# The modulation weights of a transformer block, loaded as whole megabytes two or three units ahead, and the norms' sums ahead of the units beside them

## The chip, the cores and the metric

The kernel runs on one core of a Trainium2 chip. The metric is the time of one execution on the device, in microseconds (us); a kernel's number is the median of its runs. PE is the matmul engine (TensorE), DVE is VectorE, ACT is ScalarE, POOL is GpSimd, and SP (SyncE) issues the loads. L387 is line 387 of the kernel before.

## The reference

Two blocks stand one behind the other, each of two layers, on 256 tokens `x` and 256 context tokens of width 1024. The change lies in the second block. Its first layer (i = 2 in the kernel) mixes by attention over 8 heads, its second (i = 3) by pooling over windows; both have a feed-forward part with a short convolution. Six vectors of modulation come for each layer from a matrix product of the condition `c`:

```
m = (silu(c) @ w_mod[i] + b_mod[i])           # 1024 -> 6 x 1024, also for the context's c
shift_m, scale_m, gate_m, shift_f, scale_f, gate_f = six parts of m
h = rmsnorm(x, g_pre_mix[i]) * (1 + scale_m) + shift_m
y = attention(h, hc) @ w_o    (i = 2)    or    pool_mix(h, w_pool)    (i = 3)
x = x + gate_m * rmsnorm(y, g_post_mix[i])
h = rmsnorm(x, g_pre_ffn[i]) * (1 + scale_f) + shift_f
x = x + gate_f * rmsnorm(conv_ffn(h, w_up, conv_w, conv_b, w_down), g_post_ffn[i])
```

## The kernel before

Everything is held with features on the 128 partitions: `x` is 8 tiles of 128 x 256. Weights arrive in fp32, mostly in pieces of 512 KB (`w`, L224), and are split into a high part `wh` (ACT, L238) and the rest `wl` (DVE, L240); a product is three matmuls, high by high (L285), high by low (L286 or L289) and low by high. The activations are split the same way, `hH` on ACT and `hL` on DVE or POOL (`h_tile`).

*Units.* The modulation of a layer is worked out in 24 units of 256 columns. A unit reads 1 MB of `w_mod` as two halves of 512 KB (`mod_half`, tile `mw`, three buffers, L375), multiplies it by the padded condition in 8 matmuls (L387; the trace counts 16, as fp32 goes in two passes), copies the result on ACT (`modsb`, L390), transposes it twice on PE (L396), and reduces it and adds the bias on DVE (L398, L400). `mod_units` gives a list of calls: with `ahead=1` call q issues the load of unit q and the matmuls of unit q - 1. The load is issued inside the unit, behind the copy. Units with `x8=True` take the megabyte in one DMA into a big buffer (`wm`, L366) out of a pool of seven that `y`, `sx`, the split activations and large weights share; the first block's first units are loaded so.

*Order.* The orders of PE and SP are written by hand: they are those in which the Python code issues instructions. `Line` interleaves several generators: a generator yields a cost in us, which moves a clock forward, and a wait, the time after which it is due again. The orders of ACT, DVE and POOL are set by a scheduler. All loads of weights and of units go out on SP's queue in SP's order, and SP waits at a load until the load's buffer is free.

*Where the units stand.* In the attention of layer 2 (`attention2`) 12 units of layer 3 are spread over the heads: `kx`, `vx`, `q` are the projections, `un[hp]` the scores (L1178), softmax (DVE L625, ACT L1184, DVE L1188), transposes of P (L635) and products with v (L1198) of a pair of heads. The other 12 are `self.late`; they stand beside three norms: behind the attention (post 1, five calls), behind the feed-forward of layer 2 (post 2, four) and behind the pool mixer (post 3, the rest).

*A norm* (`post_norm`) joins `rmsnorm(y)` to `x` and makes the next `h`. It needs sums over features, made by matmuls with ones: the squares of y (L449, L450) give `rstd` on ACT and DVE (L463 to L468); two more sums (L1076, of `x*y` and `y*y` with the gain, added up in `self.sx`) give the correction `m` (L1078 to L1080) to the stored sum of squares of x (L1081), and from that the second `rstd`. So h can start without a pass over the new x. `post_x` applies y to the tiles of x, five of them on POOL (L1107, L1108) and the others on DVE. In post 3 the sums of `x*y` are made in the pool mixer (L1282). `post` starts the norm's generator and runs the units beside it:

```
def post(self, units, *args):
    self.go(self.post_norm(*args), "p")
    self.run(units)
    self.line.ensure("p")
```

Of the kernel before, what the change touches and what calls it, by code (L numbers as in the profile page):

```python
# [105 lines left out]
class Stack:  # L106
# [853 lines left out]
    def ffn(self, i, T, streams, after):  # L960
# [3 lines left out]
        post = i >= 2  # L964
# [66 lines left out]
        for q in streams:  # L1031
            for ft in range(KD):
                self.go(down(len(groups) - 1, ft, slice(256 * q, 256 * q + 256)))
            after(q, nst[q], y)


# [28 lines left out]
    def post_norm(self, i, y, st, j, g):  # L1065


        nc = self.nc
        yield 0, 1.2
        ry = self.rstd(st)  # L1070
        yield 0.9, 1.5
        ps = st.get("S")
        if ps is None:
            ps = self.psum("S", [P, 2, 512])
            for n in range(2):
                nc.tensor.matmul(ps[:, n, :NT], lhsT=self.ones, rhs=self.sx[:, 1 + n], start=True, stop=True)  # L1076
        m, sx = self.t1k("m"), self.sx[:, 0]
        nc.vector.tensor_tensor(m, ps[:, 1, :NT], ry, ALU.mult)  # L1078
        nc.vector.scalar_tensor_tensor(m, ps[:, 0, :NT], 2.0, m, ALU.mult, ALU.add)
        nc.vector.tensor_tensor(m, m, ry, ALU.mult)  # L1080
        im = nc.vector.tensor_tensor(sx, sx, m, ALU.add)  # L1081
        for ft in st["pool"]:
            self.post_x(y, ry, st, ft)
        rx = self.rstd_of(sx)
        ir = self.last
        if (i, j) == (3, 3):
            self.gate = ir.ins, 1
        with self.tc.issue_after(im.ins):
            self.post_x(y, ry, st, 0)

        def pre(ft):
            if ft and ft not in st["pool"]:
                with self.tc.issue_after(ir.ins):
                    self.post_x(y, ry, st, ft)

        yield 0, 6
        yield from self.h_split(i, j, g, rx, 0, pre, POOL_H2)
        yield 0.9, 0
# [54 lines left out]
    def attention2(self):  # L1153
        nc, i, line = self.nc, 2, self.line
# [55 lines left out]
        kx, vx = chunk(0, lambda acc, s: self.post_k(acc, s, tk)), chunk(1, self.post_v)  # L1210
        q = [chunk(2 + c, post_q(c)) for c in range(4)]
        un = units()
        f = self.more_units((3, 0, 12))
        seq = kx + vx + q[0] + q[1] + need("c0", "c1", "c2") + f[:2]
        seq += spread(un[0], f[2:5]) + q[2] + need("c3") + spread(un[1], f[5:7]) + q[3] + need("c4")
        seq += spread(un[2], f[7:10]) + need("c5") + spread(un[3], f[10:])
        seq += need(*(f"a{hp}1" for hp in range(4)))
        for u in seq:
            u()
# [14 lines left out]
        for cc in range(4):  # L1234
            for f2 in range(2):
                self.go(wo(cc, f2))
        return y, nst

    def pool_consts(self):
# [11 lines left out]
    def pool_mixer(self):  # L1251
# [33 lines left out]
        nst["S"] = self.psum("S", [P, 2, 512])  # L1285
        for n in (0, 1, -1, -2, 2, -3, -4, 3, -5, -6, -7, -8):
            self.go(z(n) if n >= 0 else out(-n - 1), f"z{n}")
        line.ensure(*(f"z{-n - 1}" for n in range(KD)))
        return y, nst

# [11 lines left out]
            return self.mod_units(1, range(0, 12), True)  # L1302
        return self.more_units((2, 8, 24)) if i == 1 else []

    def more_units(self, *parts):
        return self.mod_units(None, [(i, n) for i, a, b in parts for n in range(a, b)])

    def post(self, units, *args):

        self.go(self.post_norm(*args), "p")  # L1310
        self.run(units)
        self.line.ensure("p")

    def run(self, units):
# [68 lines left out]
    def build_all(self):  # L1383
# [19 lines left out]
        if self.upto == "L1":  # L1403
            return self.finish()

        self.late = self.more_units((3, 12, 24))
        y, st = self.attention2()
        self.post(self.late[:5], 2, y, st, 3, self.sm("sm2", "n2g"))
        self.pool_consts()

        def after2(q, st, y):
            self.post(self.late[5:9], 3, y, st, 0, self.sm("sm3", "n1g"))

        self.ffn(2, 256, (0,), after2)
        if self.upto == "S0":
            return self.finish()
        y, st = self.pool_mixer()
        self.post(self.late[9:], 3, y, st, 3, self.sm("sm3", "n2g"))

        def after3(q, st, y):  # L1420
            self.go(self.post_last(y, st), "p")
# [155 lines left out]
```

## Time and profile before

| | |
|---|---|
| median of 3 runs | 1829.44 us (1826.78 to 1840.67) |
| the profiled execution | 1839.73 us |
| its span in the trace | 1837.9 us |
| mean granted clock of PE | 0.946 |
| PE busy | 1650.7 us, 90% |
| DVE, ACT, POOL busy | 64%, 49%, 7% |
| moved by DMA | 288.39 MB, 157 GB/s |
| chain that ended last | PE 65%, DVE 13%, DMA 13%, ACT 6% |
| loads of `mw`, 512 KB, x152 | median 5.0 us from issue to landing |
| loads of `wm`, 1024 KB, x20 | median 7.7 us |

The times of the trace are those of the one profiled execution, and start at its first instruction. The second block's attention lies at 1195 to 1327, post 1 behind it, post 2 at 1559 to 1585, post 3 at 1607 to 1630. The granted clock is a share of the full speed of 2.4 GHz; at any moment PE runs at this or at half of it. "Idle before <-releaser" is how long an engine stood before the instruction and what it waited for last.

### The profile page before, as it was taken

Reading aid. Unit: us, or ns where it says so; the run is one execution under the profiler, and the core shown is the slowest. Engines: PE = TensorE matmul, PEld = TensorE weight load, DVE = VectorE, ACT = ScalarE, POOL = GpSimd, SP = SyncE. Lnnn points to the kernel's source line nnn. Section 1 sums busy time; section 2 is a strip of 40 time slices with the busy share of each in tenths; the row PEclk is TensorE's granted clock in tenths of the full one; section 3 lists DMA queues with packets and bytes.
Section 4 is the critical chain, followed back from the end, with each engine's and each line's share of the span. In section 5 each row is a group of like instructions: output and inputs, shape, how many; then the busy total and the mean of one; then the engine's idle time right before and its main releaser. Section 6 shows DMA issues by size and latency. Waiting matters only on the chain.

```text
span 1837.9 us, 32872 instructions
## 1 busy us (share of the span) xinstructions
PE 1650.7 (90%) x12736; PEld 1443.7 (79%) x12736; DVE 1180.2 (64%) x2992; ACT 900.9 (49%) x2213; POOL 133.0 (7%) x162
## 2 busy tenths in 40 slices
PE   6999797999999998897799999969779999769997
PEld 5877457989889898874488888856659998459997
DVE  5665786656554567865688576746556567666665
ACT  5445554534333334554456464534446565546563
POOL 1000001000000000000001011000221012221010
PEclk9999898999999999997989999989969999789998
DMA  7334330433334332355627767465455544345552
GB/s 310 102 138 152 108 123 24 138 136 117 114 117 138 115 117 70 121 201 184 220 96 280 247 220 246 132 218 172 131 191 173 186 167 155 124 152 188 178 193 84
DMA packets 74892, 288.39 MB, mean 157 GB/s; under 512 B 8560, under 2 KB 9840, under 8 KB 69104
## 3 DMA queue, kind: packets, MB, share of 16 engines
q1 hardware_dynamic: 73152, 283.91, 45.3%
q10 hardware_dynamic: 1584, 2.38, 0.4%
q8 instruction: 100, 1.64, 0.4%
q14 instruction: 56, 0.46, 0.1%
HBM read 285.21 MB, written 1.05 MB: 156 GB/s over the span
## 4 chain that ended last, share of the span: by engine, by line
PE 65%; DVE 13%; DMA 13%; ACT 6%; issue 2%; POOL 1%; SPq 0%; ACTq 0%; DVEq 0%; POOLq 0%
PE S L285 9%; PE S L286 9%; PE S L289 9%; PE acc L285 8%; PE acc L289 8%; PE acc L286 8%; DMA mw<-in_wmod_dram 5%; DVE wl L240 4%; DMA w<-in_wup_dram 4%; PE acc L387 4%; DMA w<-in_wdn_dram 3%; ACT wh L238 2%; DVE ht L493 1%; PE tr L635 1%; PE tr L396 1%
## 5 line engine op out<-in xcount | busy, mean ns | idle before, releaser
L240 DVE TENSOR_TENSOR wl<-w,wh 128x384 fp32r<-128x384 f32 (+2 forms) x1010 | 488.0, 523 | 249.8 <-ACT wh L238 224.4
L238 ACT CAST wh<-w 128x384 fp32r<-128x384 f32 (+2 forms) x1010 | 419.8, 475 | 313.1 <-PE S L286 88.3
L285 PE MATMUL S<-hH,wh 128*128 128x256 f32 x1408 | 350.3, 286 | 20.6 <-ACT hH L503 13.6
L286 PE MATMUL S<-hL,wh 128*128 128x256 f32 x1408 | 348.4, 285 | 4.2 <-POOL hL L501 2.8
L285 PEld LDWEIGHTS S<-hH,wh 128*128 128x128 f32 x1408 | 270.7, 192 | 27.4 <-ACT hH L503 14.4
L286 PEld LDWEIGHTS S<-hL,wh 128*128 128x128 f32 x1408 | 270.5, 192 | 6.5 <-POOL hL L501 3.5
L285 PE MATMUL acc<-gH,wh 128*128 128x256 f32 (+1 forms) x728 | 209.9, 312 | 13.8 <-DVE xc L944 5.5
L286 PE MATMUL acc<-gL,wh 128*128 128x256 f32 (+1 forms) x728 | 205.3, 306 | 0.0
L289 PE MATMUL S<-hH,wl 128*128 128x256 f32 x1408 | 198.3, 284 | 0.0
L289 PEld LDWEIGHTS S<-hH,wl 128*128 128x128 f32 x1408 | 182.5, 193 | 0.0
L285 PEld LDWEIGHTS acc<-gH,wh 128*128 128x128 f32 x728 | 138.8, 191 | 29.3 <-DVE x L944 5.9
L387 PE MATMUL acc<-mw,cpad 128*32 128x256 f32 x1216 | 95.8, 427 | 60.9 <-DMA mw<-in_wmod_dram 60.4
L289 PE MATMUL acc<-gH,wl 128*128 128x256 f32 (+1 forms) x728 | 146.0, 306 | 0.0
L286 PEld LDWEIGHTS acc<-gL,wh 128*128 128x128 f32 x728 | 139.0, 191 | 5.7
L289 PEld LDWEIGHTS acc<-gH,wl 128*128 128x128 f32 x728 | 110.4, 191 | 6.5
L387 PEld LDWEIGHTS acc<-mw,cpad 128*32 128x32 f32 x1216 | 31.6, 115 | 105.9 <-DMA mw<-in_wmod_dram 51.5
L955 DVE SCALAR_TENSOR_TENSOR cgv<-S,sm,cgv 128x255 f32<-128x255 f32 (+1 forms) x132 | 74.9, 568 | 39.5 <-ACT cgv L952 39.1
L285 PE MATMUL acc<-wh,hH 128*128 128x256 f32 x344 | 92.4, 299 | 7.5 <-ACT hH L503 5.5
L390 ACT COPY modsb<-acc 128x256 f32<-128x256 f32 x96 | 35.5, 370 | 127.0 <-PE acc L387 126.3
L952 ACT ACTIVATE cgv<-S,sm 128x256 f32<-128x256 f32 (+1 forms) x132 | 82.8, 627 | 24.8 <-PE S L289 24.8
L993 POOL TENSOR_TENSOR gL<-cgv,gH 128x256 fp32r<-128x256 f32 x66 | 51.7, 783 | 543.6 <-ACT gH L992 525.7
L286 PE MATMUL acc<-wl,hH 128*128 128x256 f32 x344 | 88.6, 288 | 0.0
(261 smaller groups left out, 3011.2 us busy)
## 6 DMA issues: line engine op xcount, KB each, us to landing
mw<-in_wmod_dram SPq DMA_DIRECT2D x152, 512.0 KB, 5.0
w<-in_wup_dram SPq DMA_DIRECT2D x140, 512.0 KB, 4.1
w<-in_wdn_dram SPq DMA_DIRECT2D x56, 512.0 KB, 3.7
wm<-in_wmod_dram SPq DMA_DIRECT2D x20, 1024.0 KB, 7.7
w<-in_wup_dram SPq DMA_DIRECT2D x18, 1024.0 KB, 7.6
w<-in_win_dram SPq DMA_DIRECT2D x32, 512.0 KB, 4.2
w<-in_wout_dram SPq DMA_DIRECT2D x16, 512.0 KB, 5.5
w<-in_wqkv_dram SPq DMA_DIRECT2D x16, 512.0 KB, 4.2
```

The source lines that it names most:

```text
L238: self.nc.scalar.copy(h[:, c:d], w[:, c - a:d - a])
L240: self.nc.vector.tensor_tensor(l[:, c:d], w[:, c - a:d - a], h[:, c:d].bitcast(F32), ALU.subtract)
L285: mm(o, lhsT=s[0], rhs=m[0], start=k == ks[0], stop=False)
L286: mm(o, lhsT=s[0], rhs=m[1], start=False, stop=False)
L289: mm(o, lhsT=S(b, k)[1], rhs=M(b, k)[0], start=False, stop=end and k == ks[-1])
L387: nc.tensor.matmul(acc[32 * q:32 * q + 32], lhsT=cpad[:, k], rhs=w[k // 4][:, q], start=k < 4, stop=k >= 4)
L390: nc.scalar.copy(sb, acc)
L396: nc.tensor.transpose(tr[:, t].rearrange("p q v -> p (q v)"), sb[:, P * t:P * t + P], self.ident)
L493: nc.vector.scalar_tensor_tensor(t, self.xs[s][:, ft], A, r, ALU.mult, ALU.mult)
L952: nc.scalar.activation(out, ps, AF.Identity, scale=cw[:, n + f:n + f + 1], bias=cb[:, f:f + 1])
L955: nc.vector.scalar_tensor_tensor(o[:, :, 1:256], x[:, :, 0:255], cw[:, f:f + 1], o[:, :, 1:256], ALU.mult, ALU.add)
L993: (nc.vector if T == 512 else nc.gpsimd).tensor_tensor(gL[:, a], c[:, 1, :T], gH[:, a].bitcast(F32), ALU.subtract)
```

## The change

All 24 units of layer 3 are loaded whole, one DMA of 1 MB each, into the pool of seven big buffers. In the attention they are asked for two units ahead: the first load stands before the projection of k, the second behind that of v, and no unit's matmuls stand ahead of the first scores. The late units become three groups of four, three ahead. A group's first three loads are issued by `early_loads` at tiles 3, 4 and 5 of the loop ahead of each norm (output projection, last part of the down projection, output of the pool mixer), and its fourth in the first unit. `post` then runs the units alone. In `post_norm` the two sums have shorter waits in `Line`, which puts them earlier in PE's row. The weights, products and results are the same.

```diff
--- before.py
+++ after.py
@@ -1031,6 +1031,8 @@
         for q in streams:
             for ft in range(KD):
                 self.go(down(len(groups) - 1, ft, slice(256 * q, 256 * q + 256)))
+                if i == 2:
+                    self.early_loads(ft)
             after(q, nst[q], y)
 
 
@@ -1066,9 +1068,9 @@
 
 
         nc = self.nc
-        yield 0, 1.2
+        yield 0, 0.8
         ry = self.rstd(st)
-        yield 0.9, 1.5
+        yield 0.9, 0.8
         ps = st.get("S")
         if ps is None:
             ps = self.psum("S", [P, 2, 512])
@@ -1210,10 +1212,10 @@
         kx, vx = chunk(0, lambda acc, s: self.post_k(acc, s, tk)), chunk(1, self.post_v)
         q = [chunk(2 + c, post_q(c)) for c in range(4)]
         un = units()
-        f = self.more_units((3, 0, 12))
-        seq = kx + vx + q[0] + q[1] + need("c0", "c1", "c2") + f[:2]
-        seq += spread(un[0], f[2:5]) + q[2] + need("c3") + spread(un[1], f[5:7]) + q[3] + need("c4")
-        seq += spread(un[2], f[7:10]) + need("c5") + spread(un[3], f[10:])
+        f = self.more_units((3, 0, 12), x8=True, ahead=2)
+        seq = f[:1] + kx + vx + f[1:2] + q[0] + q[1] + need("c0", "c1", "c2")
+        seq += spread(un[0], f[2:5]) + q[2] + need("c3") + spread(un[1], f[5:8]) + q[3] + need("c4")
+        seq += spread(un[2], f[8:11]) + need("c5") + spread(un[3], f[11:])
         seq += need(*(f"a{hp}1" for hp in range(4)))
         for u in seq:
             u()
@@ -1234,6 +1236,7 @@
         for cc in range(4):
             for f2 in range(2):
                 self.go(wo(cc, f2))
+                self.early_loads(2 * cc + f2)
         return y, nst
 
     def pool_consts(self):
@@ -1285,6 +1288,8 @@
         nst["S"] = self.psum("S", [P, 2, 512])
         for n in (0, 1, -1, -2, 2, -3, -4, 3, -5, -6, -7, -8):
             self.go(z(n) if n >= 0 else out(-n - 1), f"z{n}")
+            if n < 0:
+                self.early_loads(-n - 1)
         line.ensure(*(f"z{-n - 1}" for n in range(KD)))
         return y, nst
 
@@ -1302,13 +1307,19 @@
             return self.mod_units(1, range(0, 12), True)
         return self.more_units((2, 8, 24)) if i == 1 else []
 
-    def more_units(self, *parts):
-        return self.mod_units(None, [(i, n) for i, a, b in parts for n in range(a, b)])
-
-    def post(self, units, *args):
-
+    def more_units(self, *parts, **kw):
+        return self.mod_units(None, [(i, n) for i, a, b in parts for n in range(a, b)], **kw)
+
+    def early_loads(self, ft):
+
+        if 3 <= ft < 6 and self.late:
+            self.late[0][ft - 3]()
+
+    def post(self, *args):
+
+        units = self.late.pop(0)
         self.go(self.post_norm(*args), "p")
-        self.run(units)
+        self.run(units[3:])
         self.line.ensure("p")
 
     def run(self, units):
@@ -1403,19 +1414,19 @@
         if self.upto == "L1":
             return self.finish()
 
-        self.late = self.more_units((3, 12, 24))
+        self.late = [self.more_units((3, n, n + 4), x8=True, ahead=3) for n in (12, 16, 20)]
         y, st = self.attention2()
-        self.post(self.late[:5], 2, y, st, 3, self.sm("sm2", "n2g"))
+        self.post(2, y, st, 3, self.sm("sm2", "n2g"))
         self.pool_consts()
 
         def after2(q, st, y):
-            self.post(self.late[5:9], 3, y, st, 0, self.sm("sm3", "n1g"))
+            self.post(3, y, st, 0, self.sm("sm3", "n1g"))
 
         self.ffn(2, 256, (0,), after2)
         if self.upto == "S0":
             return self.finish()
         y, st = self.pool_mixer()
-        self.post(self.late[9:], 3, y, st, 3, self.sm("sm3", "n2g"))
+        self.post(3, y, st, 3, self.sm("sm3", "n2g"))
 
         def after3(q, st, y):
             self.go(self.post_last(y, st), "p")
```

SP's row in the attention, before (-) and after (+): `wqkv` and `wo` are the weights of the projections, `wmod` those of the units.

```order
-L224 DMA w<-in_wqkv_dram 128x1024 x14
-L375 DMA mw<-in_wmod_dram 128x1024 x10
+L224 DMA w<-in_wqkv_dram 128x1024 x6
+L366 DMA wm<-in_wmod_dram 128x2048
+L224 DMA w<-in_wqkv_dram 128x1024 x4
+L366 DMA wm<-in_wmod_dram 128x2048
+L224 DMA w<-in_wqkv_dram 128x1024 x4
+L366 DMA wm<-in_wmod_dram 128x2048 x3
 L224 DMA w<-in_wo_dram 128x1024 x2
-L375 DMA mw<-in_wmod_dram 128x1024 x4
+L366 DMA wm<-in_wmod_dram 128x2048 x3
 L224 DMA w<-in_wo_dram 128x1024 x2
```

Ten half-megabyte loads stood behind all qkv weights; now two whole ones stand among these and three behind them.

PE's row in the attention before, from the last transposes of the first queries (L584) to the last unit ahead of the third query projection:

```order
L584 MATMUL tr<-cst,rp_13265 128x128 x4
L387 MATMUL acc<-mw,cpad_104 32x256 x8
L1178 MATMUL S<-kv,qT 128x512 x2
L396 MATMUL tr<-cst,modsb 128x128 x2
L387 MATMUL acc<-mw,cpad_104 32x256 x8
L1178 MATMUL S<-kv,qT 128x512 x2
L584 MATMUL tr<-cst,rp_13360 128x128 x4
L396 MATMUL tr<-cst,modsb 128x128 x2
L387 MATMUL acc<-mw,cpad_104 32x256 x16
```

And after, the same place (L1180 is the line of the scores there):

```order
L584 MATMUL tr<-cst,rp_13269 128x128 x4
L1180 MATMUL S<-kv,qT 128x512 x2
L387 MATMUL acc<-wm,cpad_104 32x256 x8
L1180 MATMUL S<-kv,qT 128x512 x2
L396 MATMUL tr<-cst,modsb 128x128 x2
L584 MATMUL tr<-cst,rp_13364 128x128 x4
L387 MATMUL acc<-wm,cpad_104 32x256 x16
```

The first scores stood behind a unit and now stand ahead of all of them; four units stood here, now three.

PE's row at post 2, before (-) and after (+), behind the last matmuls of the down projection; post 1 reads the same.

```order
-L387 MATMUL acc<-mw,cpad_104 32x256 x16
+L387 MATMUL acc<-wm,cpad_104 32x256 x8
 L449 MATMUL tr<-nacc,ones 128x256
 L450 MATMUL tr<-sq,ones 128x256
-L396 MATMUL tr<-cst,modsb 128x128 x4
-L387 MATMUL acc<-mw,cpad_104 32x256 x16
-L1076 MATMUL S<-sx,ones 128x256 x2
+L387 MATMUL acc<-wm,cpad_104 32x256 x8
+L396 MATMUL tr<-cst,modsb 128x128 x2
+L1078 MATMUL S<-sx,ones 128x256 x2
+L387 MATMUL acc<-wm,cpad_104 32x256 x8
+L396 MATMUL tr<-cst,modsb 128x128 x2
```

The sums of the squares of y stood behind two units and now stand behind one; the sums of `self.sx` stood behind two more and now stand behind one more.

## Rows read from the trace of the kernel before

**Rows 1.** stages: us, PE, PEld, DVE, ACT, POOL busy (x); clock; DMA; GB/s
```profile
1195.00:1320.00 125.00, 100.17 (x712) 75.34 (x712) 68.39 (x194) 51.10 (x130) 4.91 (x6) 0.90 0.52 173
1320.00:1368.00 48.00, 29.84 (x185) 21.13 (x184) 26.52 (x66) 20.56 (x49) 17.49 (x22) 0.70 0.58 190
```

**Rows 2.** attention, idle of PE before L387: releaser, us, times
```profile
  DMA mw<-in_wmod_dram: 21.7, 6
```

**Rows 3.** waits of PE, 1545 to 1670: releaser, us, times, longest
```profile
PE acc L387 <- DMA mw<-in_wmod_dram: 14.7, 4, 5.9
```

**Rows 4.** post 1, PE in order: start, length, instruction, [idle before <-releaser]
```profile
1333.48 2.23 PE L387 MATMUL acc<-mw,cpad 128*32 128x256 f32 x16 [5.87 <-DMA mw<-in_wmod_dram]
...
1339.67 1.22 PE L449 MATMUL tr<-nacc,ones 128*128 128x256 f32 x2
...
1356.76 0.58 PE L285 MATMUL S<-hH,wh 128*128 128x256 f32 x1 [4.82 <-ACT hH L503]
```

**Rows 5.** attention, PE in order of time
```profile
1206.36 0.60 PE L584 MATMUL tr<-cst,rp 128*128 128x128 f32 x4
1216.36 2.24 PE L387 MATMUL acc<-mw,cpad 128*32 128x256 f32 x16 [9.40 <-DMA mw<-in_wmod_dram]
1218.53 2.70 PE L1178 MATMUL S<-kv,qT 128*128 128x512 f32 x4
...
1222.38 1.99 PE L1178 MATMUL S<-kv,qT 128*128 128x512 f32 x4
...
1243.53 3.62 PE L1198 MATMUL tr<-PT,kv 128*128 128x256 f32 x16
...
1304.38 0.47 PE L285 MATMUL acc<-mixH,wh 128*128 128x256 f32 x1
```

**Rows 6.** GB/s moved, 1200 to 1260 in 40 slices
```profile
GB/s 38 314 178 175 0 177 246 210 292 385 382 52 175 287 251 197 292 216 227 322 309 328 374 303 218 11 0 0 11 0 0 5 0 74 218 333 391 333 333 347
```

**Rows 7.** attention in pieces: PE busy, granted clock, DMA share, GB/s
```profile
1216.00:1243.00 27.00, 20.75 (x144) 0.80 0.59 203
...
1264.00:1304.40 40.40, 31.77 (x206) 0.92 0.51 167
```

**Rows 8.** post 1, ACT in order of time
```profile
1329.93 0.41 ACT L437 ACTIVATE sq<-y 128x256 f32<-128x256 f32 x1
```

**Rows 9.** post 1, VectorE in order of time
```profile
1344.24 0.43 DVE L468 SCALAR_TENSOR_TENSOR rstd<-var,rstd 128x256 f32<-128x256 f32 x1
1351.13 0.42 DVE L1078 TENSOR_TENSOR m<-S,rstd 128x256 f32<-128x256 f32 x1 [6.46 <-PE S L1076]
...
1352.13 0.42 DVE L1080 TENSOR_TENSOR m<-m,rstd 128x256 f32<-128x256 f32 x1
```

**Rows 10.** post 1, GpSimd in order of time
```profile
1347.53 1.40 POOL L1107 TENSOR_TENSOR pn<-y,rstd 128x256 f32<-128x256 f32 x2
```

**Rows 11.** posts 2 and 3, PE in order of time
```profile
1566.13 2.24 PE L387 MATMUL acc<-mw,cpad 128*32 128x256 f32 x16 [5.90 <-DMA mw<-in_wmod_dram]
...
1585.06 0.58 PE L285 MATMUL acc<-wh,hH 128*128 128x256 f32 x1 [4.82 <-ACT hH L503]
...
1611.88 0.64 PE L387 MATMUL acc<-mw,cpad 128*32 128x256 f32 x8 [3.54 <-DMA mw<-in_wmod_dram]
...
1629.86 0.58 PE L285 MATMUL S<-hH,wh 128*128 128x256 f32 x1 [8.07 <-ACT hH L503]
```

**Rows 12.** posts 2 and 3, VectorE in order of time
```profile
1579.43 0.42 DVE L1078 TENSOR_TENSOR m<-S,rstd 128x256 f32<-128x256 f32 x1 [6.14 <-PE S L1076]
...
1621.27 0.17 DVE L398 TENSOR_REDUCE mod<-tr 128x4 f32<-128x16 f32 x1 [3.44 <-PE tr L396]
...
1622.35 0.94 DVE L1080 TENSOR_TENSOR m<-m,rstd 128x256 f32<-128x256 f32 x1
```

**Rows 13.** post 3, ACT in order of time
```profile
1624.74 1.23 ACT L238 CAST wh<-w 128x384 fp32r<-128x384 f32 x3 [3.44 <-DMA w<-in_wup_dram]
```

**Rows 14.** attention, SP's DMA issues in order of time
```profile
1255.58 37.17 SPq L375 DMA_DIRECT2D mw<-in_wmod_dram  x10
```

## The prediction

> **What bounds the kernel now.** I read the busy shares first, then PE's busy time stage by stage, then what PE waits for in each stage, then single instructions in order of time. The page says that PE is busy 90% of the span, so most of the 1839.7 us of the profiled execution is matmul work that this change leaves alone. The stage view shows where it is not: in the second block's attention PE works 100.2 of 125 us at a granted clock of 0.90, and in the 48 us around the norm behind it (post 1) 29.8 us at 0.70 [rows 1]. So I ask what ends the idle time there. Before the modulation matmuls (L387) of the attention PE stands six times until half a megabyte of `mw` has landed, 21.7 us in all [rows 2]. In the stretch that holds the second and third norm (posts 2 and 3) the same wait costs 14.7 us in four pieces [rows 3]. In post 1 the first piece alone is 5.87 us, and PE then stands 4.82 us more for `hH`, the output of the norm itself [rows 4]. The reader should see two things: a load that is asked for one unit ahead of its use, and behind it a norm whose sums (L449, L450, L1076) stand in PE's row after units that wait for loads. The 21.7 us sit in the attention, the rest is three times the same pattern. The feed-forward stretches between them hold no such wait, and I expect nothing there.
>
> **Attention, the waits.** The whole-megabyte loads are asked for before k's projection, after v's, and then two units ahead. PE's last projection work ends near 1206.96, the first unit starts at 1216.36, and only behind it stand the scores of the first head pair at 1218.53 [rows 5]. In the new row the scores stand first and the first unit's weights were asked for long before. All 21.7 us of load waits can go. Three things come back.
> First, what is late next. The path from the first scores to the first product with v took 25.0 us (1218.53 to 1243.53) [rows 5]: scores, maximum, exponential, the transposes of P. With 12 units and two projections no longer held up, PE reaches the transposes earlier, and the units have to hand their accumulators to ACT, which also runs the exponentials and the casts of the last qkv weights. In the new order one unit's copy stands behind both exponentials of the pair, so the next projection can wait for its accumulator. No row shows that wait. Its ends are 0 (the copies are in time) and 9.40 us (a wait as long as the first load wait) [rows 5]; I take 3.5, nearer to 0, since the work that it stands behind, two pairs of exponentials, is a few us long.
> Second, the first two megabytes now go out in front of the last eight and the last four of the qkv weight loads. The DMA view reaches 391 GB/s in its best slice [rows 6], so a megabyte takes 2.7 us of all the engines. At worst both delay a weight by their whole time, 5.4 us; at best the weights are early enough, 0. I take 1.5.
> Third, the clock. Behind a wait PE runs slow for a while: four score matmuls take 2.70 us right after the 9.40 us wait, and 1.99 a little later [rows 5]. The granted clock, a mean of its two levels of 1.2 and 2.4 GHz, is 0.80 in 1216 to 1243 and 0.92 in 1264 to 1304.4 [rows 7]: 0.20 of 27 us and 0.08 of 40.4 us, 8.6 us in all, could come back if PE never stood. Some of that is idle time counted twice, and some stands remain, so I take 4, between 0 and 8.6.
> Attention: 21.7 - 3.5 - 1.5 + 4 = 20.7 us. Its ends together would be 6.9 and 30.3; I keep 10 to 28. The output projection, which starts at 1304.38 [rows 5], then starts near 1284.
>
> **Post 1.** PE is free 5.87 us before 1333.48, at 1327.61; the first sum starts at 1339.67 [rows 4]. It needs the squares of the last tile, which ACT finishes at 1330.34 [rows 8]. With the three first loads asked for during the output projection, one unit stands in that gap (16 matmuls) and L449 can start at about 1330.4, 9.3 us earlier. Then the second sum: `rstd` is there at 1344.67, 5.0 us after L449 began, but `m` waits 6.46 us more for the sums of x at L1076 and starts at 1351.13, 11.5 us after L449 [rows 9]. Now these sums stand one unit behind L450 and are there before `rstd`, so `m` starts about 5.7 us after L449. That gives 5.8 us, and 15.1 with the first. From `m` to the first feed-forward matmul before: 1351.13 to 1356.76, 5.6 us [rows 4, 9]. This gets longer. GpSimd applies the norm to five of the tiles from `rstd` on; that was over by the time `m` began, and now runs beside the whole chain. ACT has the casts of weights and of the band that arrived before, now in front of its logarithm and of `hH`. I take 2.5 us for both, between 0 and 7 (GpSimd's five pairs of 0.7 us, [rows 10]). Post 1: 15.1 - 2.5 = 12.6 us, from 8 to 15.
>
> **Post 2.** Here the first unit is already in time; PE stops at 1560.23 and resumes at 1566.13, and L449 follows 2.2 us later [rows 11]. Squares are there 2.7 us behind the last projection matmul in post 1 (1330.34 against 1327.61), so L449 can start near 1561.9 instead of 1568.3: 6.4 us. `m` starts at 1579.43, 11.1 us after L449 [rows 12]; with 5.7 that is 5.4 us more. Less 1 us for GpSimd beside the chain: 10.8 us, from 8 to 13.
>
> **Post 3.** The sums of x are made earlier in the pool mixer, so only the first part and the loads behind it count. L449 comes 0.56 us after 1611.88, and PE had stood 3.54 us [rows 11]; that and the second unit's matmuls, which stood in front, make it 4. DVE then waits 3.44 us between the two halves of the `m` chain, for a unit's transpose that is late by its load [rows 12]. Both go: 7.4 us. The remaining stand for `hH` is 8.07 us [rows 11]; part of it is ACT, which stands 3.44 us for up-projection weights and casts them before its logarithm [rows 13]; these were queued behind unit loads that now go out earlier. I take half, 4, less 1 for GpSimd: 10.4 us, from 6 to 12.
>
> **What the new loads push aside.** SP sends its loads in one row. Three megabytes now stand among the output and up-projection weights, three among the pool and up-projection weights, and those behind the attention's units move too. With 2.7 us each [rows 6], eight of them on the path would be 21.5 us; they would cost 0 if every weight keeps its lead. I take 4. The extra wait on a buffer (four of the seven big buffers rotate here) holds SP alone, and SP has nothing else than loads behind it; I count nothing, and price the failure below.
>
> **Sum.** 20.7 + 12.6 + 10.8 + 10.4 - 4 = 50.5 us. The profiled execution, 1839.73, would become 1789. The median of the three runs, 1829.44, is 10 us lower with the same program, so I subtract from it: 1829.4 - 50.5 = 1779, 2.8% faster.
>
> **Rivals.**
> Softmax takes the place of the loads: the chain of the pairs, not the units, paces the attention. For it: the path of 25.0 us from the first scores to the first product lies behind the longest of the load waits, so at least those 25 us are not all load. Against: PE is busy through most of it. Then the first stage gives 10 in place of 20.7: 1789.
> GpSimd holds VectorE. In post 3 the same multiply took 0.94 us while GpSimd ran [rows 12], against 0.42 in post 1 with GpSimd done [rows 9]. The changed order puts the whole chain, some eight VectorE operations, beside GpSimd: 8 times 0.52 is 4.2 us for each of the three norms, 12.5 in all, of which 4.5 are counted: 1787. Against: it is one operation in one norm. The Trainium skill, SBUF — State Buffer, section "SBUF: two separate sides", says that VectorE with two SBUF inputs and a reading GpSimd take turns on one exclusive pair of ports, each for a full instruction. By that rule, every such operation could wait for a whole GpSimd one; the trace agrees for the 0.94 us.
> Weights late: all of the 21.5 us come due, because the megabytes stand ahead of loads that PE needs first: 1779 + 17.5 = 1796. For it: the DMA share is 0.52 and 0.58 in these stages [rows 1], so they are far from empty. Against: the same bytes move in any case.
> Nothing moves: the loads stay late because SP reaches them only when a buffer is given back, so units wait as before and only the order of the sums helps, 5 us a norm: 1814.
> Slower: SP stands at a unit's load until its big buffer is free, and the weights queued behind stand too. SP already spends 37.17 us on ten `mw` loads that way [rows 14], with output weights behind them. If a buffer is held by a tensor that lives through the stage, each weight load behind it is exposed with its landing and casts; at the price of the longest load wait, 9.40 us, eight of them cost 75 us, and with 50 gained the kernel would be 25 us slower: 1854. It decides when the held load stands longer than the lead of the weights behind it.
>
> **How the numbers follow.** The sum as it stands has 0.62, softmax 0.13, GpSimd 0.08, late weights 0.10, nothing moves 0.04, slower 0.03. The range takes the ends of the terms without all at once: 1760 below (attention 28, the norms at 15, 13 and 12 and nothing pushed aside give 68, 1761) and 1802 above, which holds the softmax, GpSimd and late-weights cases. One per cent, 18 us, is about what a measurement of this kernel can tell from no change: faster by more than that 0.91, within it 0.06, slower 0.03.
>
> **What would show it.** In the profile after: waits of L387 for its weights near zero in the attention and the norms (under 5 us in all); the output projection starting 15 to 25 us earlier; the first sum 2 to 4 us behind the last projection matmul of each norm; `m` right behind `rstd`; the first feed-forward matmul 12, 11 and 10 us earlier against the last matmul before each norm. The prediction is wrong if PE waits instead for `wh` or `wl`, for the accumulators' copies on ACT, or for a chain on VectorE that has grown as much as the waits have shrunk.

## The result, and the profile after

The changed kernel takes 1783.22 us (median of 4 runs, 1781.07 to 1784.92), the one before 1833.18 (4 runs, 1826.78 to 1840.67). The ratio is 0.9725, with a 95% interval of 0.9682 to 0.9769: 50 us or 2.7% faster, where 1779 was forecast, in a range of 1760 to 1802. Run again beside three of the experiments it gave 1784.65 and 0.9734 (0.9709 to 0.9759).

The profiled execution of the changed kernel is shorter by 57.3 us (span 1780.6 against 1837.9). Of these, 4.8 lie ahead of the attention's first scores, where the change hardly reaches: the transposes of the queries ahead of them begin at 1206.36 before [rows 5] and at 1201.57 after, and in the profiles of the twelve runs below anywhere from 1199.1 to 1209.8. So I compare lengths of stages, from the trace, and not points of time. Attention is from these transposes to the first matmul of the output projection; a norm is from the end of the last matmul before it to the first matmul that uses its result; all in us. The output projection, between the attention and post 1, takes 23.2 us in both kernels.

| stage | before | after | saved | again | forecast |
|---|---|---|---|---|---|
| attention | 98.0 | 74.6 | 23.4 | 24.5 | 20.7 |
| post 1 | 29.1 | 17.7 | 11.4 | 11.6 | 12.6 |
| feed-forward of layer 2 | 202.5 | 199.6 | 2.9 | 0.7 | part of -4 |
| post 2 | 25.8 | 17.3 | 8.5 | 8.5 | 10.8 |
| pool mixer | 21.9 | 21.9 | 0.0 | 0.1 | part of -4 |
| post 3 | 23.0 | 14.4 | 8.6 | 8.6 | 10.4 |
| rest | 208.1 | 210.2 | -2.1 | -0.6 | part of -4 |

"Again" is what the second profile of the changed kernel saves. Its differences from the first in the stretches without units, 2.2 and 1.6 us, are the size of what a profile leaves open there.

The attention of the changed kernel, PE in order of time; the rows answer to [rows 5]:

```profile
1201.57 0.60 PE L584 MATMUL tr<-cst,rp 128*128 128x128 f32 x4
1205.13 3.11 PE L1180 MATMUL S<-kv,qT 128*128 128x512 f32 x4 [2.96 <-DVE qT L261]
1208.17 1.58 PE L387 MATMUL acc<-wm,cpad 128*32 128x256 f32 x16
...
1223.76 3.62 PE L1200 MATMUL tr<-PT,kv 128*128 128x256 f32 x16
```

and the start of its output projection:

```profile
1276.22 0.47 PE L285 MATMUL acc<-mixH,wh 128*128 128x256 f32 x1
```

The first scores begin 3.6 us after the transposes, where it was 12.2 before, and no unit of the attention waits for a load. The first product with v comes 18.6 us behind the scores (25.0 before). What PE waits for in this stretch now, us in all, times and the longest:

```profile
PE S L1180 <- DVE qT L261: 3.0, 1, 3.0
...
PE acc L285 <- ACT modsb L390: 0.9, 1, 0.9
```

The waits for loads, 21.7 us [rows 2], are gone from the attention; in post 2 one of 1.9 us is left. PE's busy time in the stage fell too, from 73.2 to 66.6 us for the same 491 matmuls, and its idle time from 24.8 to 8.0, before and after (span, busy time, clock, DMA share, GB/s):

```profile
1206.36:1304.38 98.02, 73.19 (x491) 0.88 0.54 182
1201.57:1276.22 74.65, 66.64 (x491) 0.98 0.62 223
```

The granted clock of PE over the attention and over post 1, in the same form:

```profile
1201.00:1276.00 75.00, 67.00 (x494) 0.98 0.61 221
1299.00:1317.00 18.00, 8.31 (x84) 0.85 0.61 204
```

It is 0.98 over the attention where it was 0.80 and 0.92 in the two pieces of [rows 7], and 0.85 in post 1 where the wider stretch of [rows 1] had 0.70.

Post 1 of the changed kernel, PE, to be read against [rows 4]:

```profile
1299.39 1.07 PE L387 MATMUL acc<-wm,cpad 128*32 128x256 f32 x16
1300.39 0.70 PE L449 MATMUL tr<-nacc,ones 128*128 128x256 f32 x2
1302.63 0.70 PE L450 MATMUL tr<-sq,ones 128*128 128x256 f32 x2 [1.54 <-ACT sq L437]
...
1304.53 1.03 PE L1078 MATMUL S<-sx,ones 128*128 128x256 f32 x4
...
1317.17 0.58 PE L285 MATMUL S<-hH,wh 128*128 128x256 f32 x1 [5.28 <-ACT hH L503]
```

The last matmul ends at 1299.46. L449 stands 0.9 us behind it (12.1 before), and the sums of x (L1078, L1076 before) come at 1304.53, before they are needed. But PE then stands 5.28 us for `hH`, not less than the 4.82 before. Posts 2 and 3, PE, against [rows 11]:

```profile
1517.69 0.70 PE L449 MATMUL tr<-nacc,ones 128*128 128x256 f32 x2
...
1534.09 0.58 PE L285 MATMUL acc<-wh,hH 128*128 128x256 f32 x1 [4.55 <-ACT hH L503]
...
1556.92 0.70 PE L449 MATMUL tr<-nacc,ones 128*128 128x256 f32 x2
...
1570.40 0.58 PE L285 MATMUL S<-hH,wh 128*128 128x256 f32 x1 [5.01 <-ACT hH L503]
```

From L449 to the first feed-forward matmul it is 16.8 us in post 1, 16.4 in post 2 and 13.5 in post 3. Where this goes is seen on VectorE, here in post 1, against [rows 9]:

```profile
1307.31 0.42 DVE L1080 TENSOR_TENSOR m<-S,rstd 128x256 f32<-128x256 f32 x1
...
1308.70 0.41 DVE L1082 TENSOR_TENSOR m<-m,rstd 128x256 f32<-128x256 f32 x1
1309.15 0.83 DVE L1083 TENSOR_TENSOR sx<-sx,m 128x256 f32<-128x256 f32 x1
...
1310.77 0.81 DVE L464 TENSOR_SCALAR var<-sx 128x256 f32<-128x256 f32 x1
...
1312.37 0.94 DVE L466 SCALAR_TENSOR_TENSOR var<-var,rstd 128x256 f32<-128x256 f32 x1
...
1314.78 0.41 DVE L468 SCALAR_TENSOR_TENSOR rstd<-var,rstd 128x256 f32<-128x256 f32 x1
```

and on GpSimd beside it:

```profile
1308.71 1.85 POOL L1110 TENSOR_TENSOR x<-x,pn 128x256 f32<-128x256 f32 x2
```

`m` starts right behind `rstd`, as forecast, at 1307.31. Behind it L1083, L466 and L467 take 0.83 to 0.94 us in place of 0.42, and L464 0.81 in place of 0.28 in post 1 before (L1082 here, at 1308.70, still fell between two of GpSimd's operations; in posts 2 and 3 it takes 0.94 and 0.91). GpSimd's take 0.9 each in place of 0.7 [rows 10]. The way from `m` to the first matmul is 9.9 us, 10.5 and 9.9 in the three norms. It was 5.6, 5.6 and 12.5 (in post 3 with a load wait of 3.44 us inside, [rows 12]).

### The profile page after: what moved, and what is told of

It reads as the page before. It is cut to its first block, busy times and chain, and to the rows that moved or that the text cites. A ratio compares the mean times of both kernels' runs of the same rounds, so it can differ in the third digit from the quotient of the medians.

```text
span 1780.6 us, 32836 instructions
## 1 busy us (share of the span) xinstructions
PE 1629.6 (92%) x12736; PEld 1434.5 (81%) x12736; DVE 1190.4 (67%) x2992; ACT 900.2 (51%) x2213; POOL 136.5 (8%) x162
## 4 chain that ended last, share of the span: by engine, by line
PE 62%; DVE 16%; DMA 12%; ACT 6%; issue 2%; POOL 1%; SPq 0%; ACTq 0%; DVEq 0%; POOLq 0%
PE S L286 9%; PE S L285 9%; PE S L289 9%; PE acc L285 8%; PE acc L286 8%; PE acc L289 8%; DVE wl L240 5%; DMA w<-in_wup_dram 4%; DMA w<-in_wdn_dram 3%; PE acc L387 3%; ACT wh L238 2%; DMA mw<-in_wmod_dram 2%; DVE ht L493 2%; PE tr L635 1%; DVE mx L625 1%
## 5 line engine op out<-in xcount | busy, mean ns | idle before, releaser
L285 PE MATMUL acc<-gH,wh 128*128 128x256 f32 (+1 forms) x728 | 210.0, 312 | 14.4 <-DVE xc L944 5.5
L944 DVE SCALAR_TENSOR_TENSOR x<-acc,mod,x 128x256 f32<-128x256 f32 x104 | 50.0, 481 | 57.7 <-PE acc L289 57.3
L286 PE MATMUL S<-hcL,wh 128*128 128x256 f32 x352 | 86.5, 284 | 0.3 <-DVE hcL L504 0.3
L285 PE MATMUL S<-hcH,wh 128*128 128x256 f32 x352 | 86.4, 281 | 0.0
```

The lines of the kernel that those rows point to most:

```text
L285: mm(o, lhsT=s[0], rhs=m[0], start=k == ks[0], stop=False)
L286: mm(o, lhsT=s[0], rhs=m[1], start=False, stop=False)
L944: self.nc.vector.scalar_tensor_tensor(x, acc[:, c], self.mods(i, j)[:, ft, s:s + 1], x, ALU.mult, ALU.add)
```

## The experiments

**Which part of the change gives what.** The attention's part alone, on the kernel before:

```diff
-        f = self.more_units((3, 0, 12))
-        seq = kx + vx + q[0] + q[1] + need("c0", "c1", "c2") + f[:2]
+        f = self.more_units((3, 0, 12), x8=True, ahead=2)
+        seq = f[:1] + kx + vx + f[1:2] + q[0] + q[1] + need("c0", "c1", "c2")
...
```

> The kernel before with the attention's part of the change alone: its twelve units are loaded whole and two ahead, the late units and the norms stay as they were. If the gain is the sum of its stages, the attention gives what the trace of after shows between the last projection and the output projection, about 23 us: 1833 - 23 = 1810, with the waits of L387 in the attention near zero and post 1 unchanged (first feed-forward matmul some 29 us behind the last output projection matmul). If the attention's gain needs the later loads to be moved as well (SP free of the last units when the output and up-projection weights are due), or if part of it comes back as waits in post 1, it is 10 us or less: 1823.

Measured: 1813.4 us, ratio 0.9900 (0.9865 to 0.9935). The attention takes 73.7 us in the trace, as in the changed kernel; post 1 stays at 29.9. The gain of the attention is its own and no wait of post 1 takes it back. The time fell by 19 us where the trace of the stage says 24; the interval (12 to 25 us) holds both.

The late units alone, in the changed kernel with the attention and the waits of the sums as before:

```diff
-        yield 0, 0.8
+        yield 0, 1.2
         ry = self.rstd(st)
-        yield 0.9, 0.8
+        yield 0.9, 1.5
...
-        f = self.more_units((3, 0, 12), x8=True, ahead=2)
+        f = self.more_units((3, 0, 12))
...
```

> The changed kernel with the attention as before and with the waits of the norm's sums as before: what is left is the late units in three groups of four, loaded whole and asked for in the loops ahead of the norms. If the late loads are most of the gain at the norms, the 25 us of load waits there go and the sums, which then stand behind units that wait for nothing, come only a unit or two later than in the changed kernel: 22 to 28 us, 1805 to 1811. If the place of the sums is most of it, this gives 12 us or less: 1821 or more.

Measured: 1807.99 us, ratio 0.9868 (0.9829 to 0.9906). The norms take 18.2, 18.1 and 15.6 us, 26.0 less than before: the late loads are most of the gain at the norms. The sums alone, on the kernel before:

```diff
-        yield 0, 1.2
+        yield 0, 0.8
         ry = self.rstd(st)
-        yield 0.9, 1.5
+        yield 0.9, 0.8
```

> The kernel before with the two waits of the norm's sums alone set to 0.8 each: no load is moved. The units behind the sums still wait for their loads and stand in PE's row ahead of the first feed-forward matmul, so by the theory that the loads set the end of the row only the part of the chain behind the last unit is saved, 3 to 5 us for each norm: 1819 to 1824. If the sums are what held the norm, the chain from the sums to the first matmul moves as a whole, 8 us or more for each: 1809 or less. If the row is held by its loads alone, nothing: 1833.

Measured: 1816.44 us, ratio 0.9919 (0.9890 to 0.9949); the norms take 22.9, 21.1 and 17.9 us, 16.0 less than before, about 5 for each, at the upper end of the first case and above it in post 1. The two parts overlap: 26.0 and 16.0 alone, 28.5 together (77.9 to 49.5). How, is seen on PE in post 1. With the sums alone:

```profile
1333.72 1.22 PE L449 MATMUL tr<-nacc,ones 128*128 128x256 f32 x2
...
1338.13 1.03 PE L1076 MATMUL S<-sx,ones 128*128 128x256 f32 x4
...
1345.38 1.08 PE L387 MATMUL acc<-mw,cpad 128*32 128x256 f32 x8 [1.84 <-DMA mw<-in_wmod_dram]
...
1348.92 0.58 PE L285 MATMUL S<-hH,wh 128*128 128x256 f32 x1 [1.28 <-ACT hH L503]
```

and with the late loads alone:

```profile
1324.38 0.70 PE L449 MATMUL tr<-nacc,ones 128*128 128x256 f32 x2
...
1330.51 1.13 PE L1078 MATMUL S<-sx,ones 128*128 128x256 f32 x4
...
1340.73 0.58 PE L285 MATMUL S<-hH,wh 128*128 128x256 f32 x1 [7.92 <-ACT hH L503]
```

With the sums alone, L1076 comes 4.4 us behind L449 and the chain is under way while PE still waits for the last units' loads; their end, just ahead of 1348.92, and the chain's now come together. With the loads alone, the sums stand behind two units each, but these wait for no load, and L1078 is 6.1 us behind L449. Each part takes away most of the same wait. So the whole change without the sums' part:

```diff
-        yield 0, 0.8
+        yield 0, 1.2
         ry = self.rstd(st)
-        yield 0.9, 0.8
+        yield 0.9, 1.5
```

> The changed kernel with the waits of the norm's sums as before (1.2 and 1.5): all loads early, the sums one unit later each. The late loads alone took 27.1 us off the three norms in the trace, the sums alone 15.9, both together 28.5. By that the sums' place is worth 1 to 3 us once nothing waits for a load: 1783 + 2 = 1785. If the sums carry what the prediction gave them, 5 us or more for each of posts 1 and 2, it is 1793 or more.

(Added up rightly, the late loads alone took 26.0 us off the norms, not 27.1.) Measured: 1788.4 us, ratio 0.9777 (0.9753 to 0.9801), against 0.9725 and 0.9734 of the whole change. The norms take 51.8 us in its trace against 49.5: 2.3 us, as expected. The median is 4 to 5 us off and the ratio 8 to 10, with intervals that just overlap, and the traced execution was the fastest of its four, so the size is left open between 2 and 9 us; the stages speak for 2. The prediction counted 11 for posts 1 and 2.

Why the place is worth so little is seen on VectorE in post 1 of this run:

```profile
1307.62 0.42 DVE L1080 TENSOR_TENSOR m<-S,rstd 128x256 f32<-128x256 f32 x1 [3.04 <-PE S L1078]
```

The stand of 3.04 us for the sums is what the place removes. Over the three norms `m` comes 6.9 us sooner behind the last matmul in the changed kernel than here (19.2 against 26.1 us), but the way from `m` to the first matmul is 4.6 us longer (30.3 against 25.6): GpSimd starts at 1304.71 here, 2.9 us ahead of `m`, and in the changed kernel together with it.

**Why the attention's loads are in time.** On the kernel before, the units whole but one ahead and in the place of before:

```diff
-        f = self.more_units((3, 0, 12))
+        f = self.more_units((3, 0, 12), x8=True)
...
```

> The kernel before with the attention's units loaded whole, but still one ahead and all behind the qkv weights. If it is the depth and the early start that hide the loads, this saves little: the first wait of 9.4 us stays or grows, since the whole megabyte must land before the first matmul, and the other five waits change by a microsecond or two: 1826 to 1834, against 1813 for the attention's whole change. If it is the size, most of the 23 us comes here: 1815.

Measured: 1817.42 us, ratio 0.9927 (0.9907 to 0.9947): 2 us from the second number, the one for the size, and far from the first. What PE waits for from the attention to post 1, us, times and longest:

```profile
PE acc L387 <- DMA mw<-in_wmod_dram: 11.6, 5, 5.8
PE acc L387 <- DMA wm<-in_wmod_dram: 9.8, 1, 9.8
```

The `mw` line is post 1's, which stays. In the attention one wait of 9.8 is left of six (21.7 us, [rows 2]), and the stage takes 81.3 us, 16.7 less. The order of SP's row is that of before, with one load for two; what changed beside the size is the room. Three buffers of 512 KB hold one and a half units, four big ones that rotate hold four, so SP gets to the loads earlier. SP's issues for the first five units, before and in this run (start, time from the first to the last, count):

```profile
1208.56 20.33 SPq L375 DMA_DIRECT2D mw<-in_wmod_dram  x10
1212.12 10.42 SPq L366 DMA_DIRECT2D wm<-in_wmod_dram  x5
```

Before, three halves go out in the first 1.4 us and the fourth 8.9 us behind the first; here four whole units go out in 2.8 us and the fifth 10.1 us behind the first. "One ahead" or "two ahead" in the code hardly sets how far SP is ahead in this stage: it issues what it reaches until a buffer is missing. My two explanations, depth and size, left out the room. This run changes size and room together; the halves below part them.

The early start by itself, in the changed kernel:

```diff
-        seq = f[:1] + kx + vx + f[1:2] + q[0] + q[1] + need("c0", "c1", "c2")
+        seq = kx + vx + q[0] + q[1] + need("c0", "c1", "c2") + f[:2]
```

> The changed kernel with the attention's first two loads behind all qkv weights, where the loads of the kernel before began; the buffers, two ahead and all else stay. If the room in the big buffers hides all but the first load (one ahead and whole, all but the first wait were gone), then the first wait, up to 9 us, comes back in part: the scores no longer stand behind a unit, so only the unit between them waits for a landing near 1216, and 4 to 9 us are lost: 1788 to 1792. If the early start is worth nothing, since the softmax path is as long, it stays at 1783.

Measured: 1786.84 us, ratio 0.9762 (0.9735 to 0.9788); in the same set the changed kernel has 0.9734. The attention takes 79.5 us against 73.5 and 74.6:

```profile
PE acc L387 <- DMA wm<-in_wmod_dram: 5.5, 1, 5.5
PE S L1180 <- DVE qT L261: 1.8, 1, 1.8
```

One wait of 5.5 us for a unit is back, within the 4 to 9 expected. The time is only 2 us above that of the changed kernel and the intervals overlap, so the loss is shown in the stage and not in the time. The wait of the first scores on the copy of the queries (L261) is 1.8 us, where the first profile of the changed kernel had 3.0. It doesn't follow that the early megabytes hold up the qkv weights: the second profile of the changed kernel has 1.9, and so has the attention's part alone, which loads as early:

```profile
PE S L1178 <- DVE qT L261: 1.9, 1, 1.9
```

At this place that cost is between 0 and 1.2 us by these traces.

Size by itself: the changed kernel with two loads of 512 KB for each unit, into the same buffer and at the same place.

```diff
-            self.nc.sync.dma_start(out=w, in_=src)
+            for e in range(1 if i < 3 else 2):
+                c = slice(0, CH) if i < 3 else slice(1024 * e, 1024 * e + 1024)
+                self.nc.sync.dma_start(out=w[:, c], in_=src[:, c])
```

> The changed kernel with each unit of layer 3 loaded in two halves of 512 KB into the same big buffer, at the same place in SP's row: depth and buffers as in the change, the size as before. If depth is what counts, it stays within 3 us of the changed kernel, 1780 to 1786. If whole megabytes are what the loads gain by (fewer, longer transfers), the halves land later and 5 us or more come back: 1788 or more.

Measured: 1787.34 us, ratio 0.9763 (0.9734 to 0.9793). The norms are the same (49.7 us); the attention takes 77.5 us, 3 to 4 more. The interval overlaps that of the changed kernel, so a loss of up to 4 us is likely but not shown; most of the gain is not the size, which leaves the room for most of what whole units gained above. No unit of the attention waits for its load here either. The 3 us are a stand of PE for the first unit's copy on ACT:

```profile
PE tr L398 <- ACT modsb L392: 3.7, 1, 3.7
```

That copy stands behind a cast of a qkv weight, which came late in this profile:

```profile
1213.69 0.51 ACT L238 CAST wh<-w 128x384 fp32r<-128x384 f32 x1 [4.75 <-DMA w<-in_wqkv_dram]
```

In the changed kernel the same cast waited 2.24 us, and 1.7 in the second profile. Whether the halves made that weight late is not shown.

**What stretches the norms.** Two temporaries of the chain in PSUM, on the changed kernel:

```diff
...
-        m, sx = self.t1k("m"), self.sx[:, 0]
-        nc.vector.tensor_tensor(m, ps[:, 1, :NT], ry, ALU.mult)
-        nc.vector.scalar_tensor_tensor(m, ps[:, 0, :NT], 2.0, m, ALU.mult, ALU.add)
+        m0, m, sx = self.t1k("m"), ps[:, 1, NT:], self.sx[:, 0]
+        nc.vector.tensor_tensor(m0, ps[:, 1, :NT], ry, ALU.mult)
+        nc.vector.scalar_tensor_tensor(m, ps[:, 0, :NT], 2.0, m0, ALU.mult, ALU.add)
...
-        rx = self.rstd_of(sx)
+        rx = self.rstd_of(sx, ps[:, 0, NT:])
```

> The changed kernel with two temporaries of the norm's chain on VectorE, the second form of m and the var of the second rstd, in PSUM (the idle half of the tile that holds the sums) in place of SBUF. The work is the same. If GpSimd's reading of SBUF holds VectorE operations that read two tensors from SBUF or run in a fast form, then L1082, L1083, L464, L466 and L467 fall from 0.81 to 0.94 us to about 0.42 while GpSimd runs, some 2.5 to 3.5 us for each norm: 1783 - 9 = 1774. If they are long for another reason (the clock, the length of the queue), nothing changes: 1783.

Measured: 1779.59 us, ratio 0.9716 (0.9687 to 0.9745). VectorE in post 1:

```profile
1309.81 0.42 DVE L1082 TENSOR_TENSOR S<-S,rstd 128x256 f32<-128x256 f32 x1
...
1310.26 0.42 DVE L1083 TENSOR_TENSOR sx<-sx,S 128x256 f32<-128x256 f32 x1
1310.60 0.91 DVE L1112 SCALAR_TENSOR_TENSOR pn<-y,G,rstd 128x256 f32<-128x256 f32 x1
1311.44 0.41 DVE L464 TENSOR_SCALAR S<-sx 128x256 f32<-128x256 f32 x1
...
1312.31 0.42 DVE L466 SCALAR_TENSOR_TENSOR S<-S,rstd 128x256 f32<-128x256 f32 x1
```

The same lines as in the changed kernel now take 0.41 and 0.42 us while GpSimd runs: L1082, L1083 and L466 read one tensor from SBUF and the other from PSUM, and L464 reads one from SBUF and writes to PSUM. L1112 between them, which is not changed and reads two tensors from SBUF, still takes 0.91 (0.48 for the same operation in post 1 before). From `m` to the first matmul it is 7.7, 8.3 and 8.5 us; the norms fall from 49.5 to 43.2. Again, beside the changed kernel:

> The changed kernel with the two temporaries in PSUM, again, beside the changed kernel. The three norms were 6.2 us shorter in its trace (43.2 against 49.5 us). If that reaches the end, it is 4 to 8 us below the changed kernel of this run; if the first feed-forward matmuls give it back (their tiles still need GpSimd), 0 to 2 us.

Measured: 1778.54 us, ratio 0.9712 (0.9685 to 0.9739), 6 us below the changed kernel's 1784.65 of this set, norms 43.3 us. The medians say 6 and so does the trace; the intervals overlap, so the gain is shown in the norms and likely in the time.

GpSimd without the tiles of x, on the changed kernel:

```diff
-POOL_X = (1, 2, 3, 4, 5)
+POOL_X = ()
```

> The changed kernel with no tile of the second block's norms applied on GpSimd: VectorE applies all eight, with 10 operations more for each norm. The chain from m to the first feed-forward matmul runs without GpSimd beside it. If GpSimd's reads are what stretches it, it falls from about 10 us to 6 in each norm, and the same operations read 0.42 us; the eight tiles then come slower, 0.9 us more for each of five, so that the whole is 1779 to 1790. If the chain stays at 10 us, the stretch has another cause, and the time is 1790 or more.

Measured: 1789.97 us, ratio 0.9779 (0.9753 to 0.9806). VectorE in post 1, temporaries in SBUF as in the changed kernel:

```profile
1312.95 0.42 DVE L1082 TENSOR_TENSOR m<-m,rstd 128x256 f32<-128x256 f32 x1
1313.41 0.42 DVE L1083 TENSOR_TENSOR sx<-sx,m 128x256 f32<-128x256 f32 x1
...
1314.15 0.29 DVE L464 TENSOR_SCALAR var<-sx 128x256 f32<-128x256 f32 x1
...
1315.26 0.42 DVE L466 SCALAR_TENSOR_TENSOR var<-var,rstd 128x256 f32<-128x256 f32 x1 [0.48 <-ACT rstd L465]
```

0.42 again, and 0.29 for L464, so the stretch was GpSimd's doing. The norms take 37.6 us, 11.8 less than in the changed kernel. But the stretches that follow take more: the feed-forward of layer 2 204.4 us against 199.6, the pool mixer 24.0 against 21.9, the rest 216.0 against 210.2, 12.7 in all. PE in the first 21 us behind post 1 (span, busy time with the count of matmuls, clock, DMA share, GB/s), without GpSimd's tiles

```profile
1319.06:1340.00 20.94, 16.82 (x82) 0.66 0.19 64
```

and in the changed kernel:

```profile
1317.17:1338.00 20.83, 19.18 (x128) 0.80 0.34 112
```

82 matmuls at a clock of 0.66 in place of 128 at 0.80: the tiles of h now come one by one from VectorE, PE stands between them and stays slow for longer. What the norms gain, their readers lose. The time is 5 us above the 1784.65 measured for the changed kernel in another set, with intervals that overlap, so taking all tiles from GpSimd gains nothing, and whether it costs something is open. Between the two, with the temporaries in PSUM:

```diff
-POOL_X = (1, 2, 3, 4, 5)
+POOL_X = (3, 4, 5)
```

> The two temporaries in PSUM, and three tiles of a norm on GpSimd in place of five. If what is left of the stretch (L1112, L1113 and the tiles of h at 0.6 to 0.9 us) still costs, the norms fall by another 1 to 2 us each and the time by up to 4 us; if the tiles that VectorE then applies come late for the first feed-forward matmuls, as with no tile on GpSimd, nothing or a loss of up to 5 us. I take the second to be likelier.

Measured: 1774.92 us (1773.39 to 1777.03), ratio 0.9686 (0.9662 to 0.9709), against 0.9734 of the changed kernel beside it. The norms take 39.5 us against 43.3 with five tiles; the loss that I thought likelier didn't come. Every run is below every run of the changed kernel of its set, by 10 us in the median. Against five tiles with the same temporaries it is 4 us, and there the runs overlap: what the fewer tiles give by themselves is shown in the norms and not in the time.

The changed kernel of that set:

> The changed kernel itself once more, on the chip of the three runs beside it, so that they are compared with it and not with its first run on another chip: 1780 to 1788.

Measured: 1784.65 us.

## Why the prediction was right, step by step

The time came 4 us above the forecast, and the likeliest case was the one that happened. The saving itself is 50.0 us where 50.5 was forecast; the 4 us are the kernel before, whose median is 1829.44 with three runs and 1833.18 with a fourth. That the saving is so close is in part luck: not every term was right, and errors on either side cancelled.

*Attention, 20.7 forecast, 23.4 and 24.5 measured.* All 21.7 us of load waits went, as the step said. PE's other idle time in the stage rose by 4.9 us, from 3.1 to 8.0, where 3.5 and 1.5 were taken, but in another place: 3.0 for the first scores, which before stood behind the 9.40 us wait of a unit, and only 0.9 for the accumulators' copies, for which 3.5 was taken. What the qkv weights pay is between 0 and 1.2 us, where 1.5 was taken. The clock was taken too small: PE's busy time fell by 6.6 us for the same matmuls at 0.98 in place of 0.88 over the stage, where 4 was taken. 21.7 - 4.9 + 6.6 is the 23.4 measured. The softmax rival (10 us) fell: the first product with v came 6.4 us sooner behind the scores.

*The norms' first part.* L449 starts 0.9 us behind the last matmul in all three, sooner than 2.8: only L450 needs the last squares, and waited 1.5 us for them in post 1.

*The sums of x.* The step was right in its picture (`m` right behind `rstd`) and wrong in its account: it counted 5.8 and 5.4 us for their place, beside the loads. Most of those microseconds come with the loads alone as well (26.0 of 28.5 us); the place gives 2.3 on top by the stages, as the chain that it brings forward then runs beside GpSimd.

*From `m` to the first matmul.* Here is the term that was mis-sized. 2.5, 1 and 1 us were taken for GpSimd and the casts. The way is 4.2 us longer in post 1 and 4.9 in post 2. In post 3, where 12.5 was to fall by the load wait of 3.44 and half of the stand for `hH`, to about 6, it is 9.9. Without GpSimd's tiles it is 7.0, 6.4 and 5.8 us, against 9.9, 10.5 and 9.9, so GpSimd's part is 2.8, 4.1 and 4.1, 11 us in all. The rival that GpSimd holds VectorE, with 4.2 for a norm and a chance of 0.08, was mostly true, and should have been the forecast's own term: the row that showed it (0.94 against 0.42 us, [rows 9, 12]) was the nearest to the new place of the chain. Nor was it one operation alone; in the same norm before, also beside GpSimd, L1110 took 0.94 us, where it took 0.48 in post 1:

```profile
1624.15 0.94 DVE L1110 SCALAR_TENSOR_TENSOR pn<-y,G,rstd 128x256 f32<-128x256 f32 x1
```

GpSimd's 11 us, where 4.5 was taken for it and the casts together, are the main reason why the norms gave 28.5 us and not 33.8. The Trainium skill, SBUF — State Buffer, section "SBUF: two separate sides", lets a VectorE operation with two SBUF inputs take turns with a GpSimd operation that reads SBUF, and one in a two-port mode with any GpSimd operation. The runs agree for the first: with one of the two tensors in PSUM the operations of the chain took 0.42 us beside GpSimd, and without GpSimd's tiles 0.42 as well. For L464, with its single tensor, no run shows which mode it ran in, only that it took 0.29 us alone, 0.81 beside GpSimd and 0.41 with its output in PSUM.

*What the loads push aside.* 4 us were taken; the stretches where it would show gained 0.8 us in one profile and 0.2 in the other. The output projection kept its 23.2 us. The late-weights rival (21.5 us) fell, and so did the one in which SP is held and the kernel is slower.

Sum: 23.4 + 11.4 + 8.5 + 8.6 = 51.9 us in the four places, against 54.5 forecast for them before the 4 for what is pushed aside. The attention gave 2.7 more, the norms 5.3 less, and the 4 didn't fall due.

Left open: what the sums' place is worth between 2 us by the stages and 9 by the ratios, whether the halves made the qkv weight late that cost 3 us in the attention, and the 2 us or so by which the stretches without units differ from profile to profile.

## What to carry to other kernels

A load that has its place in the code still waits for its buffer: count the room of the pool that it goes into (here one and a half units against four; whole loads with that room gave 16.7 of some 24 us) before the depth that the code asks for. Two edits that take away the same wait don't add up: 26 and 16 us alone were 28.5 together. When a chain on VectorE is moved, look what GpSimd does at the new place: here two temporaries in PSUM were worth more to the norms (6 us) than the move of the sums (2 us).

## What the runs showed of the hardware

Beside a GpSimd multiply or add on SBUF, most of VectorE's 128 x 256 operations on two SBUF tensors took 0.83 to 0.94 us in place of 0.42 to 0.48 (some fell between two GpSimd operations and kept their time), and a tensor-scalar operation with a single SBUF tensor 0.81 in place of 0.29; the latter I had not expected. With one operand or the output in PSUM they took 0.41 to 0.43. GpSimd's operations grew as well, from 0.70 to 0.9 us.
